# The mixer's input and output projections in pairs of column chunks, a quarter of their depth by seven products

## The chip, the cores and the metric

One core of one Trainium2 chip runs the kernel. The metric is the device time of one execution in microseconds. Before the change the median of three runs is 1919.73 us (1919.63 to 1920.5). One execution was also profiled; it took 1920.29 us, and the profiler's span of it is 1918.5 us.

Engines are named as in the profile: PE is the matrix engine (PEld its weight loads), DVE the vector engine, ACT the scalar engine, POOL the engine GpSimd, SP the queue that issues most transfers.

## The reference

A decoder layer on 256 tokens of width 2048 in float32:

```python
def reference(x, mem, ...):
    x = x + 0.5 * swiglu(rms_norm(x, ffn1_norm), ...)             # d_ff 5632
    x = x + hybrid_mixer(rms_norm(x, mix_norm), ...)
    x = x + cross_attention(rms_norm(x, xattn_norm), rms_norm(mem, mem_norm), ...)
    x = x + 0.5 * swiglu(rms_norm(x, ffn2_norm), ...)

def hybrid_mixer(h, ...):
    proj = h @ w_in                       # 2048 -> 6144 columns and 16 more
    qa, ka, va, qg, kg, vg, rg, glr = split(proj)
    qa = rope(rms_norm(heads(qa)) , pos) * HEAD_DIM ** -0.5
    ka = rope(rms_norm(heads(ka)), pos)
    o_attn = dilated_attention(qa, ka, heads(va))                  # 8 heads of 128
    o_gla = rms_norm(gla_chunked(qg, kg, vg, log_a)) * silu(rg)    # 4 heads
    return concatenate([o_attn, o_gla], axis=-1) @ w_out           # 2048 -> 2048
```

Accuracy is that of float32: the kernel splits each operand into a high part (rounded for the PE) and a low part (the rest), and adds three products, high by high, low by high and high by low.

## The kernel before

**Tiles.** Activations are held transposed, as tiles of 128 partitions x 4 x 256, one for 512 of the 2048 input columns; such a tile is called a k group, and there are four. A weight matrix is cut into column chunks of 512; one chunk of one k group is a load of 1 MB (`load`). ACT casts it to the high part `wh`, DVE subtracts to get the low part `wl` (`wsplit`; line 145 in the profile). A matmul multiplies 128x128 activations (the 256 tokens are two halves, t = 0 and 1) by 128x512 weights, so one chunk of one k group takes 24 matmuls: 4 rows of the group, 2 halves of the tokens, 3 products.

**Stages.** The two feed-forward stages and the middle (mixer and cross-attention) have separate memory pools. In the middle a load is split as two halves of 128x1024, with WB = 4 buffers for `wh` and as many for `wl`; in the feed-forward stages a load is split whole.

**Two ways to multiply.** `proj` (lines 175 to 177) takes one column chunk over its four k groups, 96 matmuls into two accumulators in PSUM. `strassen` (lines 219 and 184), used by the feed-forward stages alone, takes two column chunks at once. For two of the k groups the product of a 2x2 block matrix (two k groups by two chunks on the weights' side, two k groups by two token halves on the other) is formed by seven products rather than eight, from sums of weights and sums of activations (`sums_of`); the other k groups are added in the ordinary way (`whole`). The seven products run in a fixed order, P1 to P7. P1 goes into the tile `x`, P2 into `y`; ACT copies `x` to the first accumulator (`c0l`) and `y` to a tile `ys` in SBUF. P3 is added onto `x`, then DVE writes the accumulator `c0r = ys - x`. P4 is added to `c0l`. P5 is added onto `x`, so it has to wait until DVE has read `x`; then DVE writes `c1r = ys - x`. P6 is added to `c0r` and P7 onto `x`, again after that second reading.

**What sets the order.** A scheduler turns the program into a fixed list for each engine when the kernel is built; each engine works its list from the front. Weight loads and splits, and the copies and subtractions in `strassen`, are moved ahead of other work by 200 places where their operands and buffers allow. Steps between the projections (transposes, scores, softmax, attention) are put off with `later(n, step)`: each step runs after n ticks, and a tick is counted after half a k group in `proj`, after each product and twice in `whole`.

**Buffers.** [...] Short-lived tiles in SBUF, 2 KB in a partition each, come from one pool of SB = 6 buffers (`W2`): `ys`, and in the rotary step of a projection the tiles `sq`, `un`, `t1` and `t2`.

**The rotary step** (`roped`, lines 742 to 773, with `head_scale`, lines 448 to 462). For each token half of each query or key chunk, ACT squares the accumulator (`sq`), DVE reduces and scales it, POOL raises it to the power -1/2 (line 359), DVE multiplies (`qf` or `kf`), ACT scales the accumulator with it (`un`, four instructions), DVE and POOL make two products (`t2`, `t1`), DVE adds them (`qn`). Each instruction needs the one before.

The column chunks of `w_in` in the order worked on before: 6 and 7 (gated queries and keys), 8 and 9 (gated values), 10 and 11 (output gate), 0, 2, 1, 3 (query, key, query, key), 4 and 5 (values). The keys of the memory follow, then `w_out` in four chunks, k groups in the order 2, 3, 0, 1.

Of the kernel before, what the change touches and what calls it, by code (L numbers as in the profile page):

```python
# [29 lines left out]
WB = 4  # L30
PR0 = 10
PR1 = 9
ATT = 4
# [3 lines left out]
SCI = 1  # L37
ROPE = 8
XPRI = 170
MEM0 = 2  # L40
MEMS = 3
UB = 44
SB = 6
# [6 lines left out]
def layer_kernel(ctx: ExitStack, tc: tile.TileContext, A: dict, out: bass.AP):  # L50
# [144 lines left out]
    def new_sums():  # L195
        return tuple(FT(n, 1, [P, 2, 4, S], F32R, n) for n in ("sh", "sl"))

    def sums_of(ga, gb):

        t0, t1 = slice(0, P), slice(P, S)  # L200
        sums = new_sums()
        fa, fb = (FT("h", 8, [P, 4, S], F32, n) for n in ("fa", "fb"))
        for f, (h, l) in ((fa, ga), (fb, gb)):
            V.tensor_add(f, h.bitcast(F32), l.bitcast(F32))
        V.tensor_sub(fb[:, :, t1], fa[:, :, t1], fb[:, :, t1])
        V.tensor_sub(fa[:, :, t1], fa[:, :, t0], fa[:, :, t1])
        V.tensor_sub(fa[:, :, t0], fb[:, :, t1], fa[:, :, t0])
        V.tensor_add(fb[:, :, t0], fb[:, :, t0], fa[:, :, t0])
        for i, f in enumerate((fa, fb)):
            split(*(x[:, i] for x in sums), f)  # L210
        return sums

    def product(acc, lhs, w, start):

        wh, wl = w
        first = start
        for i, j, w in ((0, 0, wh), (1, 0, wh), (0, 1, wl)):
            for k in range(4):
                PE.matmul(acc, lhs(k)[i], w[:, k], start=first, stop=j == 1 and k == 3, skip_group_check=not start)  # L219
                first = False  # L220
        tick()

    def strassen(Wl, cl, Wr, cr, lhs, ab, sums, groups, mid=None, last=False):

        a, b = ab
        ral, rar = load(Wl, cl, a), load(Wr, cr, a)
        rbr, rbl = load(Wr, cr, b), load(Wl, cl, b)

        def parts(src):
            with tc.high_priority(WPRI):  # L230
                wh, wl = (FT(x, FWB, [P, 4, 512], F32R, x) for x in ("wh", "wl"))
                wsplit(wh, wl, src)
            return wh, wl
# [8 lines left out]

        def of(g, t):
            return lambda k: lhs(4 * g + k, t)

# [25 lines left out]
        if mid:  # L271
            mid()
        accs = ((c0l, x), (c0r, c1r))
        for i, g in enumerate(groups):
            end = i == len(groups) - 1
            for j, (acc, W, c) in enumerate(zip(accs, (Wl, Wr), (cl, cr))):
                if last and end and j:
                    both = [w for half in wgroup(W, c, g) for w in half]
                    for t in range(TT):
                        mm3(acc, lhs, both, False, True, (t,), seeded=True)  # L280
                    break
                both = [w for half in wgroup(W, c, g) for w in half]
                whole(acc, lhs, both, end)
                if i == j == 0:
                    product(x, of(b, 1), parts(ral), False)
# [360 lines left out]

    later(1, k_turn)
    later(3, gated_scores)
    later(4, kd_turn)

# [43 lines left out]

    for p2 in range(2):
        acc = proj(win, 8 + p2, lhs_x, range(4))
        for t in range(TT):
            SC.activation(vg[p2][t], acc[t], AF.Copy, scale=r2[:, t:t + 1])
        later(1, lambda p2=p2: states(p2))
        later(3, lambda p2=p2: outputs(p2))  # L700

# [12 lines left out]

    for p2 in range(2):
        acc = proj(win, 10 + p2, lhs_x, range(4))
        o2s = []
        for t in range(TT):
# [9 lines left out]
            o2s.append(o2)  # L728
        later(2, lambda p2=p2, o2s=o2s: gate_turn(p2, o2s))

# [11 lines left out]

    def roped(which, g, i, c):
        acc = proj(win, c, lhs_x, range(4))
        qns = []
# [26 lines left out]

        later(ROPE, turn)

# [44 lines left out]

    def values(g):  # L820
        acc = proj(win, 4 + g, lhs_x, range(4))
# [5 lines left out]
        later(ATT, lambda: attend(g, va))  # L827

# [5 lines left out]

    roped("q", 0, 0, 0)
    roped("k", 0, 1, 2)
    later(ROPE + SCD, lambda: scores(0, 0))
    later(ROPE + SCD + SCI, lambda: scores(0, 2))
    roped("q", 1, 0, 1)
    later(PR0, lambda: probs_turn(0))  # L840
    roped("k", 1, 1, 3)
    later(ROPE + SCD, lambda: scores(1, 0))
    later(ROPE + SCD + SCI, lambda: scores(1, 2))

# [61 lines left out]
    ss3 = new_ss("ss3")  # L906
    for c in range(NC):
        acc = proj(A["w_out"], c, lhs_m, (2, 3, 0, 1))
        for t in range(TT):
            V.tensor_add(xs[c][:, t], acc[t], xs[c][:, t])  # L910
        norm_chunk(c, xs[c], 32, ss3)
    r3 = rstd_of(ss3, "r3")
# [169 lines left out]
```

## Time and profile before

| | |
|---|---|
| median of the runs | 1919.73 us |
| profiled execution | 1920.29 us |
| its span | 1918.5 us |
| PE busy | 1890.5 us, 99% of the span |
| DVE busy | 1459.3 us, 76% |
| ACT busy | 1080.1 us, 56% |
| POOL busy | 125.7 us, 7% |
| the chain that ended last | PE 93%, DVE 4%, ACT 1% |
| mean granted PE clock | 0.995 |

The mixer and the cross-attention's projections lie between 713 and 1170 us of the span. In a row of a timeline the first number is the start in us, the second the time until the end of the last of the merged instructions; matmuls overlap, so the pace of a run of them is the difference of starts. In the rows of a table by windows each engine has its busy time and, in brackets, its instructions.

### The profile page before, as it was taken

The page shows a single profiled execution, that of the slowest core. Times are in us where ns is not written, and L with a number is a line of the kernel's source. Part 1 is how long each engine was busy: PE and PEld are TensorE (multiplying, and loading weights), DVE is VectorE, ACT ScalarE, POOL GpSimd, SP SyncE. Part 2 cuts the span into 40 slices and gives each one's busy share as a digit, 9 for nine tenths or more (in the row PEclk, how much of TensorE's full clock was granted, in tenths as well). Part 3 has the DMA queues.
Part 4 walks back from the last instruction along what each step waited for, and adds up shares of the span by engine and source line. Part 5 has one row for each costly group of instructions (what it writes and reads, how often), then busy time and mean ns, then how long its engine had stood idle before and what let it go on. Part 6 is the DMA issues. An engine that isn't in the chain of part 4 may idle for free.

```text
span 1918.5 us, 21566 instructions
## 1 busy us (share of the span) xinstructions
PE 1890.5 (99%) x8616; PEld 1563.4 (81%) x8616; DVE 1459.3 (76%) x1159; ACT 1080.1 (56%) x1028; POOL 125.7 (7%) x137
## 2 busy tenths in 40 slices
PE   8999999999999999999999999899999999999998
PEld 6888888888888778778888889788888888888876
DVE  7779887788888885446785555777888878888886
ACT  6556655555555556444676445555655556556553
POOL 2000000000000000002230000000000000000000
PEclk9999999999999999999999999899999999999999
DMA  9776787777877754445465554668768777787775
GB/s 376 274 244 225 241 301 280 275 240 241 277 246 274 250 157 174 169 158 194 174 221 200 195 193 157 254 198 293 231 230 285 259 275 272 246 284 233 242 253 171
DMA packets 68480, 453.90 MB, mean 237 GB/s; under 512 B 7675, under 2 KB 8827, under 8 KB 15004
## 3 DMA queue, kind: packets, MB, share of 16 engines
q1 hardware_dynamic: 56284, 370.74, 49.2%
q0 software_dynamic: 10944, 79.70, 18.5%
q10 hardware_dynamic: 1152, 2.10, 0.3%
q8 instruction: 67, 1.10, 0.2%
q14 instruction: 33, 0.27, 0.0%
HBM read 379.10 MB, written 6.29 MB: 201 GB/s over the span
## 4 chain that ended last, share of the span: by engine, by line
PE 93%; DVE 4%; issue 1%; ACT 1%; DMA 1%; POOL 0%; SPq 0%; DVEq 0%; POOLq 0%; ACTq 0%
PE acc L184 24%; PE x L219 17%; PE acc L176 9%; PE acc L177 9%; PE acc L175 9%; PE acc L219 9%; PE x L184 8%; PE y L219 4%; DVE wl L145 2%; ACT wh L145 1%; PE tp L383 1%; DVE raw L237 1%; DMA xr<-in_xT_dram 0%; DMA raw<-raw 0%; PE tp L343 0%
## 5 line engine op out<-in xcount | busy, mean ns | idle before, releaser
L145 DVE TENSOR_TENSOR wl<-raw,wh 128x2048 fp32r<-128x2048 f32 (+2 forms) x523 | 1013.6, 1954 | 367.1 <-ACT wh L145 366.7
L145 ACT CAST wh<-raw 128x2048 fp32r<-128x2048 f32 (+2 forms) x523 | 852.2, 1640 | 621.3 <-DVE raw L237 182.2
L175 PE MATMUL acc<-wh,xTh 128*128 128x512 f32 x544 | 216.3, 399 | 9.0 <-ACT wh L145 8.8
L176 PE MATMUL acc<-wl,xTh 128*128 128x512 f32 x544 | 214.9, 395 | 4.6 <-DVE wl L145 4.6
L177 PE MATMUL acc<-wh,xTl 128*128 128x512 f32 x544 | 214.2, 394 | 0.0
L237 DVE TENSOR_TENSOR raw<-raw 128x2048 f32<-128x2048 f32 x64 | 146.5, 2290 | 1.7
L241 POOL DMA_DIRECT2D raw<-raw x64 | 55.0, 860 | 1201.2 <-ACT sg L420 473.8
L175 PEld LDWEIGHTS acc<-wh,xTh 128*128 128x128 f32 x544 | 103.1, 190 | 32.4 <-ACT wh L145 10.5
L176 PEld LDWEIGHTS acc<-wl,xTh 128*128 128x128 f32 x544 | 103.6, 190 | 28.0 <-DVE wl L145 6.9
L184 PE MATMUL acc<-wl,xTh 128*128 128x512 f32 x480 | 121.8, 389 | 0.0
L184 PE MATMUL acc<-wh,xTl 128*128 128x512 f32 x480 | 121.8, 389 | 0.0
L184 PE MATMUL acc<-wh,xTh 128*128 128x512 f32 x480 | 121.8, 389 | 0.0
L177 PEld LDWEIGHTS acc<-wh,xTl 128*128 128x128 f32 x544 | 103.6, 190 | 21.7
L184 PEld LDWEIGHTS acc<-wl,xTh 128*128 128x128 f32 x480 | 90.1, 188 | 18.7
L184 PEld LDWEIGHTS acc<-wh,xTh 128*128 128x128 f32 x480 | 90.1, 188 | 18.7
L184 PEld LDWEIGHTS acc<-wh,xTl 128*128 128x128 f32 x480 | 90.1, 188 | 18.7
L219 PE MATMUL x<-wh,sh 128*128 128x512 f32 x256 | 71.2, 400 | 3.3 <-ACT wh L145 1.9
L219 PE MATMUL x<-wh,sl 128*128 128x512 f32 x256 | 68.8, 390 | 0.0
L219 PE MATMUL x<-wl,sh 128*128 128x512 f32 x256 | 68.7, 390 | 0.0
L420 ACT ACTIVATE sg<-acc,r 128x512 f32<-128x512 f32 x24 | 16.3, 689 | 84.7 <-PE acc L184 84.7
L184 PE MATMUL acc<-wh,hTl 128*128 128x512 f32 x232 | 59.2, 390 | 2.4 <-DVE hTl L303 2.4
L184 PE MATMUL acc<-wh,hTh 128*128 128x512 f32 x232 | 59.2, 390 | 0.9 <-ACT wh L145 0.9
(339 smaller groups left out, 2828.3 us busy)
## 6 DMA issues: line engine op xcount, KB each, us to landing
raw<-in_ffn_w_up_dram SPq DMA_DIRECT2D x88, 1024.0 KB, 8.9
raw<-in_ffn_w_down_dram SPq DMA_DIRECT2D x88, 1024.0 KB, 7.6
raw<-in_ffn_w_gate_dram SPq DMA_DIRECT2D x85, 1024.0 KB, 7.8
raw<-raw POOLq DMA_DIRECT2D x64, 1024.0 KB, 6.9
raw<-in_w_in_dram SPq DMA_DIRECT2D x48, 1024.0 KB, 4.8
raw<-in_w_out_dram SPq DMA_DIRECT2D x16, 1024.0 KB, 4.8
sl<-ffn_sl POOLq DMA_DIRECT2D x4, 1024.0 KB, 9.4
sh<-ffn_sh POOLq DMA_DIRECT2D x4, 1024.0 KB, 13.3
```

The costliest lines, as they stand in the source:

```text
L145: return SC.copy(wh, src), V.tensor_sub(wl, src, wh.bitcast(F32))
L175: PE.matmul(acc[t], lh, wh, start=first and i == 0, stop=False, skip_group_check=seeded)
L176: PE.matmul(acc[t], lh, wl, start=False, stop=False, skip_group_check=seeded)
L177: PE.matmul(acc[t], ll, wh, start=False, stop=last and i == len(half) - 1, skip_group_check=seeded)
L184: PE.matmul(acc[t], lhs(w[0], t)[i], w[1 + j], start=False, stop=last and j == 1 and n == len(group) - 1, skip_group_check=True)
L219: PE.matmul(acc, lhs(k)[i], w[:, k], start=first, stop=j == 1 and k == 3, skip_group_check=not start)
L237: V.tensor_add(dst, x, y)
L241: G.dma_start(dst, x, accum_op=ALU.add)
L383: PE.transpose(tp[:, j], hs[t][:, j * P:(j + 1) * P], ident)
L420: SC.activation(s, gate[t], AF.Silu, scale=r[:, t:t + 1])
```

## The change

Chunks of `w_in` are worked on in pairs by `strassen`: (8, 9), (10, 11), (0, 2), (1, 3), (4, 5); chunks 6 and 7 stay with `proj`. `w_out` is done in the pairs (0, 1) and (2, 3). Below these are the vg pair, the gate pair, the first and the second head pair, the value pair, the first and the second output pair. Unlike in the feed-forward stages, the 2x2 block matrix is made of the two halves of one k group, group 0, so each of the seven products has 6 matmuls; the other three groups follow with `whole`. P7 is done ahead of the first `whole` here. The activations' sums for `w_in` are made once, those for `w_out` from the attention's output of the first four heads. One of the additions of weights is made by an accumulating transfer, as in the feed-forward stages, the other three by DVE. `roped` and `values` get finished accumulators, four of them at the end of each pair, and the ticks of the later steps are set anew; the pool of long-lived tiles has 40 buffers rather than 44.

```diff
-PR0 = 10
-PR1 = 9
-ROPE = 8
+PROBS = 21
+ROPEQ = 9
+ROPEK = 12
-UB = 44
+UB = 40
...
     def strassen(Wl, cl, Wr, cr, lhs, ab, sums, groups, mid=None, last=False):
-        a, b = ab
-        ral, rar = load(Wl, cl, a), load(Wr, cr, a)
-        rbr, rbl = load(Wr, cr, b), load(Wl, cl, b)
+        large = phase["half_step"]
+        if large:
...
+        else:
+            rar, ral = load(Wr, cr, ab), load(Wl, cl, ab)
+            rbr, rbl = rar[:, 2:], ral[:, 2:]
+            rar, ral = rar[:, :2], ral[:, :2]
+            a, b, m = 4 * ab, 4 * ab + 2, 2
...
-        accumulate(ral, rbl)
+        if large:
+            accumulate(ral, rbl)
+        else:
+            add(ral, ral, rbl)
...
+        if not large:
+            product(x, of(b, 1), parts(ral), False)
         for i, g in enumerate(groups):
...
-    later(1, k_turn)
-    later(3, gated_scores)
-    later(4, kd_turn)
+    later(2, k_turn)
+    later(6, gated_scores)
+    later(7, kd_turn)
...
+    xsums = sums_of(*halves(*xT[0]))
+    def pair(cl, cr):
+        return strassen(win, cl, win, cr, lhs_x, 0, xsums, (1, 2, 3))
-    for p2 in range(2):
-        acc = proj(win, 8 + p2, lhs_x, range(4))
+    for p2, acc in enumerate(pair(8, 9)):
...
-    roped("q", 0, 0, 0)
-    roped("k", 0, 1, 2)
...
+    for g in range(2):
+        for i, acc in enumerate(pair(g, 2 + g)):
+            roped("qk"[i], g, i, acc)
+        later(ROPEK + SCD, lambda g=g: scores(g, 0))
+        later(ROPEK + SCD + SCI, lambda g=g: scores(g, 2))
+        later(PROBS, lambda g=g: probs_turn(g))
...
-    values(0)
-    later(PR1, lambda: probs_turn(1))
-    values(1)
+    for g, acc in enumerate(pair(4, 5)):
+        values(g, acc)
...
-    for c in range(NC):
-        acc = proj(A["w_out"], c, lhs_m, (2, 3, 0, 1))
+    msums = sums_of(mT[0, "h", 0], mT[0, "h", 2])
+    for c in range(0, NC, 2):
+        accs = strassen(A["w_out"], c, A["w_out"], c + 1, lhs_m, 0, msums, (2, 3, 1))
```

The lists of three engines at the start of the second head pair, right after the first head pair. Lines of the changed kernel stand some 15 to 20 further down than before: 451 is now 466, 750 is 770, 758 is 778, 219 is 220, and the copy to `ys` and the first subtraction, 260 and 264, are 270 and 274. Numbers behind a name tell one tile from another.

ACT, before, at the rotary step of chunk 0 (the accumulators are `acc_6015` for t = 0 and `acc_6016` for t = 1):

```order
L451 ACTIVATE sq_6171<-acc_6015 128x512
L145 CAST wh_6271<-raw_6253 128x1024
L750 ACTIVATE un_6182<-acc_6015,qf_6180 128x128 x4
L451 ACTIVATE sq_6194<-acc_6016 128x512
L145 CAST wh_6289<-raw_6287 128x1024
L145 CAST wh_6305<-raw_6287 128x1024
L750 ACTIVATE un_6205<-acc_6016,qf_6203 128x128 x4
L145 CAST wh_6323<-raw_6321 128x1024
```

ACT now, from the cast for P6 of the second head pair (`wh_6531`) on; `acc_6050` and `acc_6051` are the key accumulators of the first head pair, and `ys_6495` is the copy of P2 of the second:

```order
L145 CAST wh_6531<-raw_6463 128x1024
L145 CAST wh_6541<-raw_6465 128x1024
L145 CAST wh_6553<-raw_6551 128x1024
L770 ACTIVATE un_6405<-x_6047,qf_6403 128x128 x4
L466 ACTIVATE sq_6417<-acc_6050 128x512
L770 ACTIVATE un_6428<-acc_6050,kf_6426 128x128 x4
L466 ACTIVATE sq_6440<-acc_6051 128x512
L770 ACTIVATE un_6451<-acc_6051,kf_6449 128x128 x4
L270 COPY ys_6495<-y_6468 128x512
```

Before, at most one chunk's two rotary halves stood together in ACT's list, with casts between them. Now those of a query and a key chunk stand together, three of the four behind the casts of all products, and the copy to `ys` stands behind the last of them.

DVE now, at the same place; `acc_6470` is `c0r` of the second head pair:

```order
L476 TENSOR_SCALAR kf_6426<-kr_6424,r2_4798 128x4
L778 TENSOR_TENSOR t2_6435<-un_6428,tab_6037 128x4x64 x2
L468 TENSOR_REDUCE ks_6442<-sq_6440 128x4
L780 TENSOR_TENSOR qn_6438<-t1_6433,t2_6435 128x512
L471 TENSOR_SCALAR km_6444<-ks_6442,r2sq_4804 128x4
L472 TENSOR_SCALAR km_6444<-km_6444 128x4
L476 TENSOR_SCALAR kf_6449<-kr_6447,r2_4798 128x4
L778 TENSOR_TENSOR t2_6458<-un_6451,tab_6038 128x4x64 x2
L274 TENSOR_TENSOR acc_6470<-ys_6495,x_6467 128x512
```

The subtraction that makes `c0r` is new at this place and stands behind the rotary work of all four halves. On PE the list is P1, P2, P3, P4, two matmuls of the first `whole`, nine transposes of rotary results, and then P5 on `x_6467`, which needs that subtraction; everything later on PE stands behind P5.

More of the change, by code (lines that the diff above doesn't have):

```diff
@@ L195, in new_sums @@
     def new_sums():
-        return tuple(FT(n, 1, [P, 2, 4, S], F32R, n) for n in ("sh", "sl"))
+        return tuple(FT(n, 1, [P, 2, 4 if phase["half_step"] else 2, S], F32R, n) for n in ("sh", "sl"))
     def sums_of(ga, gb):
@@ L201, in sums_of @@
         sums = new_sums()
-        fa, fb = (FT("h", 8, [P, 4, S], F32, n) for n in ("fa", "fb"))
+        fa, fb = (FT("h", 8, [P, 4, S], F32, n) if phase["half_step"] else U([P, 2, S], F32, n) for n in ("fa", "fb"))
         for f, (h, l) in ((fa, ga), (fb, gb)):
@@ L217, in product @@
         for i, j, w in ((0, 0, wh), (1, 0, wh), (0, 1, wl)):
-            for k in range(4):
-                PE.matmul(acc, lhs(k)[i], w[:, k], start=first, stop=j == 1 and k == 3, skip_group_check=not start)
+            m = w.shape[1]
+            for k in range(m):
+                PE.matmul(acc, lhs(k)[i], w[:, k], start=first, stop=j == 1 and k == m - 1, skip_group_check=not start)
                 first = False
@@ L283, in strassen @@
                 whole(acc, lhs, both, end)
-                if i == j == 0:
+                if large and i == j == 0:
                     product(x, of(b, 1), parts(ral), False)
@@ L713, in gate_turn @@
             mT[2 + p2, t] = (hi, lo)
-    for p2 in range(2):
-        acc = proj(win, 10 + p2, lhs_x, range(4))
+    for p2, acc in enumerate(pair(10, 11)):
         o2s = []
@@ L741, in layer_kernel, with roped @@
     pn = {}
-    def roped(which, g, i, c):
-        acc = proj(win, c, lhs_x, range(4))
+    def roped(which, g, i, acc):
         qns = []
@@ L771, in turn @@
                 T[which, g, h0] = dst
-        later(ROPE, turn)
+        later(ROPEK if i else ROPEQ, turn)
     def scores(g, h0):
@@ L818, in attend, with values @@
             mT[g, "h", h0] = (hi, lo)
-    def values(g):
-        acc = proj(win, 4 + g, lhs_x, range(4))
+    def values(g, acc):
         va = []
@@ L826, in values @@
             va.append(v_)
-        later(ATT, lambda: attend(g, va))
+        later(ATT + 2 * g, lambda: attend(g, va))
     def lhs_m(k, t):
@@ L906, in layer_kernel @@
     ss3 = new_ss("ss3")
-    for c in range(NC):
-        acc = proj(A["w_out"], c, lhs_m, (2, 3, 0, 1))
-        for t in range(TT):
-            V.tensor_add(xs[c][:, t], acc[t], xs[c][:, t])
-        norm_chunk(c, xs[c], 32, ss3)
+    msums = sums_of(mT[0, "h", 0], mT[0, "h", 2])
+    for c in range(0, NC, 2):
+        accs = strassen(A["w_out"], c, A["w_out"], c + 1, lhs_m, 0, msums, (2, 3, 1))
+        for d, acc in zip((c, c + 1), accs):
+            for t in range(TT):
+                V.tensor_add(xs[d][:, t], acc[t], xs[d][:, t])
+            norm_chunk(d, xs[d], 32, ss3)
     r3 = rstd_of(ss3, "r3")
```

25 lines of the change are left out of this document (12 added, 13 removed).

## The prediction

> **What bounds the kernel now.** I read the page first (span, busy shares, chain), then the middle of the span by windows, since only that part changes.
>
> ```profile
> span 1918.5 us, 21566 instructions
> PE 1890.5 (99%) x8616; PEld 1563.4 (81%) x8616; DVE 1459.3 (76%) x1159; ACT 1080.1 (56%) x1028; POOL 125.7 (7%) x137
> PE 93%; DVE 4%; issue 1%; ACT 1%; DMA 1%; POOL 0%; SPq 0%; DVEq 0%; POOLq 0%; ACTq 0%
> 713.00:892.00 179.00, 178.65 (x839) 144.40 (x838) 96.88 (x115) 95.61 (x125) 13.14 (x14) 1.00 0.49 173
> 892.00:1040.00 148.00, 148.00 (x700) 124.01 (x699) 106.22 (x188) 95.22 (x168) 30.71 (x24) 1.00 0.56 199
> 1040.00:1085.00 45.00, 45.00 (x208) 37.44 (x207) 26.97 (x34) 23.62 (x37) 2.71 (x3) 1.00 0.50 188
> 1085.00:1170.00 85.00, 85.00 (x440) 72.89 (x439) 50.58 (x60) 43.33 (x61) 2.71 (x3) 1.00 0.53 186
> ```
>
> PE is the bound, and in the middle it has no gap at all: 456.65 of 457 us busy. DVE is busy for 281 of the same 457 us. So a matmul removed is time gained, one for one, and any wait that the change puts in front of PE is time lost, one for one.
>
> **The gain.** Seven pairs each replace 8 x 6 matmuls by 7 x 6, so 42 matmuls fewer, which is also the difference of the two programs' lists. Their pace:
>
> ```profile
> 706.28 1.98 PE L184 MATMUL acc<-wh,hTh 128*128 128x512 f32 x8
> 709.91 1.98 PE L184 MATMUL acc<-wl,hTh 128*128 128x512 f32 x8
> 916.41 1.03 PE L768 MATMUL tp<-ident,qn 128*128 128x128 f32 x8
> ```
>
> Sixteen matmuls start in 3.63 us, 0.227 us each: 42 x 0.227 = **9.5 us gained**. (Eight transposes take about 1.03 us, 0.13 each, used below.)
>
> [...]
>
> **What is added**, and whether DVE can carry it:
>
> ```profile
> L145 DVE TENSOR_TENSOR wl<-raw,wh 128x1024 fp32r<-128x1024 f32 x12 | 14.5, 1218 | 4.0 <-ACT wh L145 4.0
> L237 DVE TENSOR_TENSOR raw<-raw 128x2048 f32<-128x2048 f32 x64 | 146.5, 2290 | 1.7
> L264 DVE TENSOR_TENSOR acc<-ys,x 128x512 f32<-128x512 f32 x32 | 22.0, 688 | 2.0 <-PE x L219 2.0
> L345 DVE TENSOR_TENSOR xg<-tp,gain 128x512 f32<-128x512 f32 x24 | 16.0, 684 | 3.3 <-PE tp L343 3.3
> raw<-raw POOLq DMA_DIRECT2D x64, 1024.0 KB, 6.9
> ```
>
> A pair adds on DVE three weight additions (half of 2.29, say 1.15 each), three splits (1.22) and two subtractions (0.69): 8.5 us; ACT three casts and two copies. Seven pairs and the two sets of sums make about 68 us: 281 + 68 = 349 of 448. On average DVE isn't the bound. The accumulating transfer needs 6.9 us at twice the size and is wanted only at P5; it is hidden by P1 to P4 and the whole group ahead, and the loads through SP are the same in number.
>
> It is at the start of a pair that it matters. There PE takes 6 matmuls a product, 1.36 us, while DVE needs 1.7 us and more (13.4 for seven), and at that moment the previous pair's four accumulators come due together. So I followed each start by hand, along the lists of the engines, with the durations of the rows. Time 0 is when P1 could start; the first two accumulators of the pair before are ready one `whole` earlier, at -5.4.
>
> **The head pairs (the largest term).** The rotary step's chain, in the profile at chunk 0 (ACT, DVE, POOL in turn):
>
> ```profile
> 893.54 0.60 ACT L451 ACTIVATE sq<-acc 128x512 f32<-128x512 f32 x1 [0.36 <-PE acc L177]
> 896.88 1.14 ACT L750 ACTIVATE un<-acc,qf 128x128 f32<-128x128 f32 x4 [0.99 <-DVE qf L461]
> 903.98 1.14 ACT L750 ACTIVATE un<-acc,qf 128x128 f32<-128x128 f32 x4 [2.59 <-DVE qf L461]
> ...
> 898.06 1.86 DVE L758 TENSOR_TENSOR t<-un,tab 128x256 f32<-128x256 f32 x2
> 899.84 0.67 DVE L453 TENSOR_REDUCE qs<-sq 128x4 f32<-128x512 f32 x1
> 900.44 0.68 DVE L760 TENSOR_TENSOR qn<-t,t 128x512 f32<-128x512 f32 x1
> 901.04 1.21 DVE L145 TENSOR_TENSOR wl<-raw,wh 128x1024 fp32r<-128x1024 f32 x1
> 902.17 0.22 DVE L456 TENSOR_SCALAR qm<-qs,r2sq 128x4 f32<-128x4 f32 x1
> 907.73 3.49 DVE L145 TENSOR_TENSOR wl<-raw,wh 128x1024 fp32r<-128x1024 f32 x3
> ...
> 902.67 1.01 POOL L359 TENSOR_TENSOR qr<-qm,mhalf 128x4 f32<-128x4 f32 x1 [3.04 <-DVE qm L457]
> ```
>
> From the end of one `un` (898.02) to the end of the next (905.12) pass 7.1 us; without the split between them (1.13 from start to start) a round is 6.0. It is a chain of waits through three engines, and ACT's and DVE's lists hold nothing else there now. At the start of the second head pair DVE first has, from -5.3 on, eight splits (1.16), three additions (1.15), two reductions and one `qn` (0.6), one `t2` (1.87) and small ones (0.6): 17.1 us, with some waits done at about 12.5. Then the second query half's `un` ends at 15.4, the key's at 21.4 and 27.4, its `t2` at 29.3; only now comes the subtraction that frees `x`, done at 30.0. P5, and all of PE behind it, starts at 30.1. PE has by then 26 matmuls (5.9) and nine transposes (1.2) to do: **23 us stalled**. At the start of the value pair the lists read the same; score work replaces part of the early rotary work, the first `t2` starts at 11, the subtraction ends at 31.5, and PE has 7.5 us of work: **24 us**. Below, were nothing but the two key halves in the way (0.6 + 0.7 + 0.4 + 1.0 + 0.3 + 1.1, one round, `t2` and subtraction), P5 would start at 12.7 and 5.6 us be lost each time. Above, with a split in each round, 27.
>
> **The output pairs.** The first needs `msums`, and DVE makes them behind the memory keys' normalisation. From -0.4: two reductions, one addition, three splits, twice the small ones with POOL's power (1.7), two additions of 512 (0.6), four of 256 (0.36, half of the row of `xg` and a little) and a cast (0.6): done at 12.3. PE has P1 and P4 alone, 2.7: **10 us** (0 if the sums came before the keys' work, 11 with one more split). At the second, `c0r` stands behind four residual additions (0.68), three weight additions, eight splits, four `xg` and three low parts (0.68): 20.2 + 0.7 from -5.3, done at 15.6; PE has 24 + 2 matmuls and 16 transposes, 8.0: **7.5 us** (0 to 9).
>
> **The other three.** The vg pair waits for `xsums`, behind five splits, three additions and two products: the second sum is there at about 8, PE has 2.7: **5 us** (0 to 6). At the gate pair `c0r` comes after six splits and three additions, at 8.6 against 6.9, and the states' products wait another turn of splits: **3 us** (0 to 4). At the first head pair eight gate products of 0.6 push P7's split to 13 against 10.8: **3 us** (0 to 5).
>
> **The clock.** After a stall PE comes back at half speed:
>
> ```profile
> 1211.60 1.91 PE L343 MATMUL tp<-ident,x 128*128 128x128 f32 x16
> 1216.80 1.22 PE L175 MATMUL acc<-wh,xTh 128*128 128x512 f32 x2 [3.29 <-ACT wh L145]
> 1220.75 0.79 PE L176 MATMUL acc<-wl,xTh 128*128 128x512 f32 x1 [2.73 <-DVE wl L145]
> 1226.46 0.43 PE L175 MATMUL acc<-wh,xTh 128*128 128x512 f32 x1
> 1216.00:1220.00 4.00, 1.22 (x2) 0.50 (x2) 4.00 (x6) 2.83 (x4) 0.04 (x1) 0.54 1.02 430
> ```
>
> Between the starts at 1220.75 and 1226.46 lie 13 matmuls in 5.71 us instead of 2.95: 2.8 us lost. The two head stalls and the two at the output pairs are longer than the 3.29 us here: 4 x 2.8 = **11 us** (0 to 14).
>
> [...]
>
> **Sum.** -9.5 + 23 + 24 + 10 + 7.5 + 5 + 3 + 3 + 11 = +77. On the profiled execution's 1920.29 that is 1997; the median shown is 0.6 lower: **1996 us**. With all stalls at their lower ends, -9.5 + 11.2, no loss could be measured; I take the middle values because they are the lists' own order, and the low ends need DVE or ACT to do work in an order that their lists don't have.
>
> The moved steps cost what they did. Transposes and scores of the heads are 9 to 14 ticks on, inside the next pair; the memory's loads, 16 on SP, and their splits end inside the value pair, and the attention of the second four heads comes six ticks into the memory keys. Should that cover go, `attend` would stand in front of PE for its operands; I allow 0 to 10 us for it in the range alone.
>
> **Rivals.**
>
> *Only the rotary stalls.* The starts of the other five pairs hide behind splits made ahead, as the same scheme does in the feed-forward stages. Then -9.5 + 47 + 5.6 = +43: 1963 us. For it speaks this row of PE's waits:
>
> ```profile
> PE x L219 <- DVE acc L264: 0.8, 4, 0.2
> ```
>
> Thirty-two starts there cost P5 and P6 0.8 us in all. Against it: there a product has 12 matmuls, 2.7 us, and no sums are made in front of it. 20%.
>
> *Faster: every start hides.* If `ys` and the subtraction are ready when P3 is, as in that row, only the gain is left: 1920.3 - 9.5 = 1910.8, 1910 on the median. It decides from the point where all stalls together stay under 9.5 us. Against it stand the lists, in which the subtraction is behind four rounds of the chain. 5%.
>
> *Longer: attention comes late as well.* The head stalls push the scores, and the second four heads' attention meets the memory keys' end; another 15 to 20 us, about 2014. Against: six ticks of cover. 5%.
>
> *DVE becomes the bound of the whole middle*: 349 of 448 us busy says no; that the change doesn't do what it says: the 42 matmuls are gone from the list. 2% together, near no change.
>
> **How the numbers follow.** Forecast 68%, 1996 us, own range 1975 to 2014; the others as given. For eight in ten I reach down past 1963 to 1955 and up to 2015. A measurement of this kernel can tell 0.2%, some 4 us, from no change: slower than that 93%, within it 2%, faster 5%.
>
> **What would show it.** In the new trace PE should have two idle stretches of over 20 us altogether, after the first and the second head pair, released by DVE's subtraction (line 274), with ACT's `ys` copy directly behind the last `un`; one of about 10 us at the first output product with sums, released by ACT's cast to `sh`; smaller ones at the other starts; and the granted clock near 0.5 behind each. 42 matmuls fewer at 0.227. I'm wrong if PE's P5 in the head pairs starts within 10 us of P4, if the middle is as full as before, or if PE comes back from the stalls at full speed.

## The result, and the profile after

The changed kernel takes 2004.16 us (median of 4 runs, 2002.29 to 2006.06) against 1919.68 us of the kernel before on the same chip (4 runs, 1918.78 to 1920.5): a ratio of 1.044, 95% interval 1.0422 to 1.0458. The forecast was 1996 us, slower. The profiled execution took 2002.29 us, its span is 2000.5 us, 82.0 more than before.

The page of the changed kernel: span, busy shares, the chain that ended last.

```profile
span 2000.5 us, 21720 instructions
PE 1903.0 (95%) x8574; PEld 1564.1 (78%) x8574; DVE 1523.0 (76%) x1231; ACT 1108.2 (55%) x1067; POOL 138.0 (7%) x144
PE 84%; DVE 8%; ACT 3%; issue 2%; DMA 1%; POOL 1%; SPq 0%; ACTq 0%; DVEq 0%; POOLq 0%
```

PE has 42 instructions fewer, as foretold, and is still busy for 12.5 us more: that alone says that it ran slower for a while. The middle, cut by windows (PE, weight loads, DVE, ACT, POOL, granted clock):

```profile
766.00:800.00 34.00, 25.13 (x110) 19.72 (x111) 25.74 (x31) 17.03 (x21) 0.00 (x0) 0.85 0.43 140
800.00:875.00 75.00, 75.00 (x326) 57.51 (x326) 37.72 (x40) 36.30 (x55) 2.91 (x3) 1.00 0.48 164
930.00:975.00 45.00, 24.35 (x93) 18.31 (x92) 30.82 (x41) 18.92 (x35) 10.94 (x9) 0.73 0.32 106
1000.00:1048.00 48.00, 25.41 (x101) 19.35 (x100) 32.68 (x53) 24.80 (x48) 18.35 (x13) 0.72 0.34 116
1107.00:1131.00 24.00, 14.91 (x62) 11.26 (x61) 18.04 (x28) 14.30 (x23) 2.01 (x2) 0.86 0.29 95
```

The first row is the start of the vg pair, the second holds the start of the gate pair without a gap, the next two are the starts of the second head pair and of the value pair, the last that of the first output pair. With the last 748.5 us of both spans set apart, the middle from 713 on lasts 539 us instead of 457. Between the same two instructions, the first matmul of line 175 (at 713.45 before, 712.23 now) and the first of the cross-attention's scores (at 1172.48 and 1255.50), it lasts 84.2 us longer; the stages ahead and behind are 2.2 us shorter this time.

PE's timeline at the starts; in square brackets the idle time ahead and what ended it. The rows at 931.57, 1003.65, 1107.52 and 1162.02 are P1 of four pairs.

```profile
771.39 1.22 PE L220 MATMUL acc<-wh,xTh 128*128 128x512 f32 x2 [5.66 <-ACT acc L264]
777.76 0.49 PE L220 MATMUL x<-wh,sh 128*128 128x512 f32 x1 [3.45 <-ACT sh L145]
...
887.89 1.22 PE L220 MATMUL x<-wh,sh 128*128 128x512 f32 x2 [3.38 <-ACT acc L264]
...
931.57 0.62 PE L220 MATMUL x<-wh,xTh 128*128 128x512 f32 x2
...
947.54 0.48 PE L788 MATMUL tp<-ident,qn 128*128 128x128 f32 x1 [4.09 <-ACT un L770]
...
959.86 0.47 PE L788 MATMUL tp<-ident,qn 128*128 128x128 f32 x1 [7.72 <-ACT ys L270]
961.86 1.22 PE L220 MATMUL x<-wh,sh 128*128 128x512 f32 x2 [1.52 <-DVE acc L274]
...
1003.65 0.62 PE L220 MATMUL x<-wh,xTh 128*128 128x512 f32 x2
...
1020.79 0.90 PE L822 MATMUL tp<-ident,pc 128*128 128x128 f32 x3 [8.07 <-ACT un L770]
1033.11 0.90 PE L822 MATMUL tp<-ident,pc 128*128 128x128 f32 x3 [11.42 <-ACT ys L270]
1035.11 0.80 PE L220 MATMUL x<-wh,sh 128*128 128x512 f32 x1 [1.10 <-DVE acc L274]
...
1107.52 0.62 PE L220 MATMUL x<-wh,mTh 128*128 128x512 f32 x2
...
1119.78 0.79 PE L220 MATMUL x<-wh,sh 128*128 128x512 f32 x1 [7.88 <-ACT sh L145]
...
1162.02 0.61 PE L220 MATMUL x<-wh,mTh 128*128 128x512 f32 x2
...
1172.79 1.09 PE L358 MATMUL tp<-ident,x 128*128 128x128 f32 x4 [4.50 <-DVE xg L360]
```

Added up with the smaller ones, PE is idle for 71.7 us in the middle: 9.1 at the vg pair, 0 at the gate pair, 4.1 and 20.6 at the two head pairs, 22.6 at the value pair, 9.1 and 5.9 at the output pairs, 0.3 elsewhere. Why it is so late at the second head pair stands in ACT's timeline there:

```profile
946.34 1.14 ACT L770 ACTIVATE un<-x,qf 128x128 f32<-128x128 f32 x4 [4.17 <-DVE qf L476]
952.27 1.14 ACT L770 ACTIVATE un<-acc,kf 128x128 f32<-128x128 f32 x4 [4.30 <-DVE kf L476]
...
958.19 1.14 ACT L770 ACTIVATE un<-acc,kf 128x128 f32<-128x128 f32 x4 [4.30 <-DVE kf L476]
959.21 0.60 ACT L270 COPY ys<-y 128x512 f32<-128x512 f32 x1
```

The rounds of the rotary chain follow each other at 5.9 us, and the copy to `ys`, whose operand P2 left in PSUM at about 934.5, comes straight behind the last `un`, 25 us later. Little of PE's idle time there is ended by the subtraction of line 274 itself (1.5 us here, 1.1 at the value pair). Most lies at the transposes ahead of P5, and the last of those wait for the copy to `ys` too (7.7 and 11.4 us), though they don't read `ys`. They write to a buffer in PSUM, one of four of the kernel's pool `pm`, from which `x` and `y` come too, so it must be the one of `y` that they wait for; that is inferred.

### The profile page after: what moved, and what is told of

Its sections match the earlier page's. It is cut to its first block, busy times and chain, and to the rows that moved or that the text cites. A ratio compares the mean times of both kernels' runs of the same rounds, so it can differ in the third digit from the quotient of the medians.

```text
span 2000.5 us, 21720 instructions
## 1 busy us (share of the span) xinstructions
PE 1903.0 (95%) x8574; PEld 1564.1 (78%) x8574; DVE 1523.0 (76%) x1231; ACT 1108.2 (55%) x1067; POOL 138.0 (7%) x144
## 3 DMA queue, kind: packets, MB, share of 16 engines
q0 software_dynamic: 11952, 83.37, 18.8%
## 4 chain that ended last, share of the span: by engine, by line
PE 84%; DVE 8%; ACT 3%; issue 2%; DMA 1%; POOL 1%; SPq 0%; ACTq 0%; DVEq 0%; POOLq 0%
PE acc L184 30%; PE x L220 18%; PE x L184 10%; PE acc L220 9%; PE y L220 4%; DVE wl L145 3%; PE acc L176 3%; PE acc L177 3%; PE acc L175 3%; ACT wh L145 2%; DVE raw L247 2%; PE tp L398 1%; DVE t L778 1%; DMA raw<-raw 1%; DMA xr<-in_xT_dram 1%
## 5 line engine op out<-in xcount | busy, mean ns | idle before, releaser
L247 DVE TENSOR_TENSOR raw<-raw 128x2048 f32<-128x2048 f32 (+1 forms) x85 | 173.0, 2036 | 2.0
L184 PE MATMUL acc<-wh,xTh 128*128 128x512 f32 x660 | 170.6, 392 | 2.8 <-ACT wh L145 2.8
L184 PE MATMUL acc<-wl,xTh 128*128 128x512 f32 x660 | 168.2, 390 | 0.0
L184 PE MATMUL acc<-wh,xTl 128*128 128x512 f32 x660 | 167.5, 389 | 0.0
L184 PEld LDWEIGHTS acc<-wh,xTh 128*128 128x128 f32 x660 | 123.7, 188 | 29.1 <-ACT wh L145 3.6
L184 PEld LDWEIGHTS acc<-wh,xTl 128*128 128x128 f32 x660 | 123.9, 188 | 25.8
L184 PEld LDWEIGHTS acc<-wl,xTh 128*128 128x128 f32 x660 | 123.7, 188 | 25.9 <-issue 0.4
L220 PE MATMUL x<-wh,sh 128*128 128x512 f32 x284 | 83.7, 411 | 21.7 <-ACT sh L145 11.3
L175 PE MATMUL acc<-wh,xTh 128*128 128x512 f32 x224 | 89.3, 403 | 6.2 <-ACT wh L145 6.2
L176 PE MATMUL acc<-wl,xTh 128*128 128x512 f32 x224 | 90.0, 402 | 5.1 <-DVE wl L145 5.1
L177 PE MATMUL acc<-wh,xTl 128*128 128x512 f32 x224 | 89.4, 399 | 0.0
L220 PEld LDWEIGHTS x<-wh,sh 128*128 128x128 f32 x284 | 51.8, 192 | 36.3 <-ACT sh L145 12.5
L220 PEld LDWEIGHTS x<-wl,sh 128*128 128x128 f32 x284 | 53.9, 191 | 12.3 <-DVE wl L145 1.0
L220 PEld LDWEIGHTS x<-wh,sl 128*128 128x128 f32 x284 | 54.2, 191 | 11.7
L435 ACT ACTIVATE sg<-acc,r 128x512 f32<-128x512 f32 x24 | 16.3, 689 | 84.7 <-PE acc L184 84.7
```

The source lines that it names most:

```text
L175: PE.matmul(acc[t], lh, wh, start=first and i == 0, stop=False, skip_group_check=seeded)
L176: PE.matmul(acc[t], lh, wl, start=False, stop=False, skip_group_check=seeded)
L177: PE.matmul(acc[t], ll, wh, start=False, stop=last and i == len(half) - 1, skip_group_check=seeded)
L184: PE.matmul(acc[t], lhs(w[0], t)[i], w[1 + j], start=False, stop=last and j == 1 and n == len(group) - 1, skip_group_check=True)
L247: V.tensor_add(dst, x, y)
L435: SC.activation(s, gate[t], AF.Silu, scale=r[:, t:t + 1])
```

## The experiments

All times are medians of four runs, each beside runs of the kernel before on the same chip. From each kernel's profiled execution the table also has PE's idle time in the middle, the time there at a granted clock of 0.50 (the middle cut into windows of 0.25 us) and half of PE's busy time in it, an estimate of what half speed cost. Where an edit adds lines of code, the later ones stand further down: line 247 is 251 in the kernels with early sums.

| kernel | us | against before | PE idle | at half speed | lost by it |
|---|---|---|---|---|---|
| changed kernel | 2004.2 | +84.5 | 71.7 | 78.5 | 16.1 |
| `ys` in its own buffer | 1991.0 | +71.4 | 53.1 | 68.3 | 22.6 |
| head chunks one by one | 1964.2 | +44.6 | 35.7 | 41.0 | 12.5 |
| output chunks one by one | 1985.1 | +65.5 | 55.3 | 64.9 | 14.2 |
| own `ys`, raw copies | 1975.6 | +56.0 | 43.4 | 44.4 | 13.6 |
| sums early | 1989.9 | +70.8 | 56.8 | 68.3 | 16.7 |
| raw copies alone | 1987.7 | +68.6 | 51.9 | 61.4 | 17.4 |
| all mended | 1947.4 | +28.3 | 18.8 | 23.9 | 11.0 |
| POOL's work moved | 1937.6 | +18.8 | 17.1 | 13.7 | 4.6 |
| four pairs | 1936.5 | +17.8 | 14.0 | 13.7 | 5.0 |
| ticks set anew | 1946.0 | +26.1 | 20.5 | 27.3 | 11.0 |

### The buffer of `ys`

```diff
-UB = 40
+UB = 39
-            ys = W2([P, 512], "ys")
+            ys = W2([P, 512], "ys") if large else FT("ys", 1, [P, 512], F32, "ys")
```

> The changed kernel, but the copy ys has a buffer of its own instead of one of the six short-lived ones (the long-lived pool has 39 buffers instead of 40; that alone leaves every engine's list as it was). Theory: the stalls at the second head pair and the value pair (20.6 and 22.6 us of idle PE) exist because ys needs a buffer that the rotary step of the fourth half frees, so that the subtraction of line 274 stands behind all four rounds. With its own buffer P5 needs only the accumulator of the first half, and what is left is the wait of the second subtraction for the third half, some 8 us at each start: 2004.2 - 12.6 - 14.6 - 5 of half speed = about 1972 us. Rival: the four accumulators themselves are freed too late by the chain of rounds, and the place of ys is only a symptom. Then another wait takes over, the two idle stretches keep 17 us and more each, and the time stays at 1995 us or above.

1991.02 us, ratio 1.0368 (1.0353 to 1.0384). The buffer is a cause: idle PE falls to 10.6 us at the second head pair and 10.2 at the value pair. At the second head pair the copy to `ys` and then P5 now come here (P1 starts at 931.51):

```profile
936.29 0.62 ACT L270 COPY ys<-y 128x512 f32<-128x512 f32 x1
```

```profile
941.17 0.71 PE L220 MATMUL x<-wh,sh 128*128 128x512 f32 x2
```

What is left in PE's timeline:

```profile
959.14 1.22 PE L220 MATMUL x<-wh,xTh 128*128 128x512 f32 x2 [3.91 <-DVE acc L282]
...
1021.31 1.22 PE L220 MATMUL x<-wh,xTh 128*128 128x512 f32 x2 [5.42 <-DVE acc L282]
...
1106.68 0.80 PE L220 MATMUL x<-wh,sh 128*128 128x512 f32 x1 [10.69 <-ACT sh L145]
```

P7 now waits for the second subtraction (line 282), which needs the accumulator of the third rotary half: the wait foretold by the theory. But the time fell by 13 us and not by 32. The first output pair's wait for its sums grew by 2.8 us, and a new one of 2.0 us came up at the memory keys; and half speed costs 6.5 us *more* although PE is idle 18.6 us less: more of PE's work now falls into the slow stretches (45.2 us of it, twice the 22.6, against 32.2). The size was wrong, the rival (1995 us and above) too.

### The head chunks one by one

```diff
-        for i, acc in enumerate(pair(g, 2 + g)):
-            roped("qk"[i], g, i, acc)
+        for i in range(2):
+            roped("qk"[i], g, i, proj(win, 2 * i + g, lhs_x, range(4)))
```

with the ticks of the kernel before for the transposes and scores (8, 9, 10), and 18 for the attention's transposes.

> The changed kernel, but the four query and key chunks go through proj one by one as before; vg, gate, value and output pairs stay. Theory: the rotary work of four accumulators at once is what costs; the first and second head pair's stalls (4.1 and 20.6 us) go, the value pair keeps a wait for the two halves of one key chunk, some 6 us instead of 22.6, about 10 us of half speed go, and two pairs' gain of 1.4 us each is lost: 2004.2 - 4.1 - 20.6 - 16.6 - 10 + 2.7 = about 1956 us. Rival: a pair's own start (three additions and seven splits on DVE) costs what it costs whatever stands ahead; then the value pair keeps 15 us and more, and the time is 1970 us or above.

1964.24 us, ratio 1.0231 (1.0216 to 1.0246), 40 us less than the changed kernel. With the head chunks no wait above 0.25 us is left. The value pair, now behind one key chunk, keeps 10.9 us, most of it in this row:

```profile
994.87 0.90 PE L822 MATMUL tp<-ident,pc 128*128 128x128 f32 x3 [6.81 <-ACT ys L270]
```

The wait for `ys` is still there with two rotary halves ahead instead of four. The theory holds but for this, which it had at 6 us, and the time is 8 us above its 1956.

### The output chunks one by one

```diff
-    msums = sums_of(mT[0, "h", 0], mT[0, "h", 2])
-    for c in range(0, NC, 2):
-        accs = strassen(A["w_out"], c, A["w_out"], c + 1, lhs_m, 0, msums, (2, 3, 1))
+    for c in range(NC):
+        acc = proj(A["w_out"], c, lhs_m, (2, 3, 0, 1))
```

> The changed kernel, but the four chunks of w_out go through proj as before; all input pairs stay. Theory: the output pairs' stalls (9.1 and 5.9 us, with some 4 us of half speed behind them) are their own: the sums of the attention's output for the first, the residual additions and the norm for the second. They go, two gains of 1.4 us are lost: 2004.2 - 15 - 4 + 2.7 = about 1988 us. Rival: these stalls are handed down from the attention that comes late after the head pairs, and proj would wait there as well: 1998 us or above.

1985.08 us, ratio 1.034 (1.0323 to 1.0357): 19.1 us less than the changed kernel, 16 foretold. With `proj` no wait above 0.25 us is left there; the output pairs' stalls are their own.

### Own `ys`, and raw copies of the accumulators

The edit of `ys` above, and in the rotary step:

```diff
+            qn = U([P, 4, HD], F32, "qn")
+            with tc.high_priority(WPRI):
+                SC.copy(flat, acc[t])
-            f = head_scale(acc[t], r2, r2sq, t, ...)
+            f = head_scale(flat, r2, r2sq, t, ...)
...
             V.tensor_add(qn, t1, t2.rearrange("p h s d -> p h (s d)"))
+            for h in range(4):
+                SC.activation(qn[:, h], qn[:, h], AF.Copy, scale=f[:, h:h + 1])
```

where `flat` is `qn` in two dimensions.

> As the first kernel of this set (ys has its own buffer), and the rotary step first copies the raw accumulator to SBUF with one ACT copy of 128x512, ahead of other work; squares and rotary products read that copy, and the normalising factor is applied at the end instead of the beginning. The arithmetic is the same but for the order of two multiplications; each half has one ACT copy more. Theory: both reasons for the late P5 and P7 (the buffer of ys, and accumulators held for whole rounds) are gone, the second head pair and the value pair lose nearly all their 43 us of idle PE and some 8 us of half speed: about 1957 us. Rival: DVE's own work at a pair's start (13.4 us for the weights of seven products against 9.5 us of PE) holds P5 to P7 whatever the accumulators do; then 5 us and more stay at each start and the time is 1965 us or above.

1975.56 us, ratio 1.0291 (1.0276 to 1.0306). The second head pair keeps 3.6 us of idle PE, the value pair's P1 to P7 0.9. Then comes another wait:

```profile
1021.67 0.90 PE L790 MATMUL tp<-ident,qn 128*128 128x128 f32 x3 [6.70 <-ACT qn L782]
```

Transposes of the rotary result stand in PE's list where the finished result is not there yet, with `whole` behind them. So neither theory nor rival is whole: the two reasons for the late P5 and P7 were right, and the chain, still as long, met PE at its next customer; the time is above the rival's 1965, but not for its reason. The wait for the output sums again grew, to 10.82 us.

### Raw copies alone

The edit of the rotary step without that of `ys`.

> The changed kernel with the raw copy of the accumulators alone (squares and rotary products read a copy in SBUF, the factor is applied at the end), ys stays in the pool of six short-lived buffers. It parts the two reasons that the fourth kernel took away together (1975.6 us; ys alone 1991.0). Theory: both are needed: the short-lived buffers turn over with the rotary rounds, three per half, and ys is still the thirteenth request behind the first, so P5 still stands behind the rounds; gain under 15 us: 1990 us or above. Rival: with the accumulators copied the rounds are short enough that ys gets its buffer in time, and the time is within 4 us of the fourth kernel's, about 1976 us.

1987.72 us, ratio 1.0357 (1.0342 to 1.0373). This edit alone gains 16.4 us, that of `ys` alone 13.1, both 28.6: near the sum, 29.6. In idle PE they overlap more: 18.6 and 19.8 us less alone, 28.3 together. Neither the theory's 1990 nor the rival's 1976 came. At the second head pair (P1 at 932.79) the copy to `ys` and P5 come here:

```profile
949.61 0.56 ACT L270 COPY ys<-y 128x512 f32<-128x512 f32 x1
```

```profile
952.23 1.22 PE L220 MATMUL x<-wh,sh 128*128 128x512 f32 x2
```

Behind P1 there, P5 and P7 start after:

| kernel | P5, us | P7, us |
|---|---|---|
| changed kernel | 30.3 | 35.0 |
| `ys` in its own buffer | 9.7 | 27.6 |
| raw copies alone | 19.4 | 24.0 |
| both | 9.6 | 13.7 |

So P5 is late for the buffer of `ys`, which the shorter hold of the accumulators frees only in part; with that mended, P7 is late for the accumulators. The two are not links of which both are needed, as the theory had it.

### The sums early

The sums for `w_in` are made after the gated queries. Those for `w_out` are made right behind the value pair, of k group 2:

```diff
-        accs = strassen(A["w_out"], c, A["w_out"], c + 1, lhs_m, 0, msums, (2, 3, 1))
+        accs = strassen(A["w_out"], c, A["w_out"], c + 1, lhs_m, 2, msums, (3, 0, 1))
```

> The changed kernel, but the sums of activations are made earlier: those for w_in after the gated query chunk instead of after the gated keys, those for w_out from k group 2 (the gate's output, ready long before) instead of group 0, with the order of the groups 2, 3, 0, 1. Nothing else differs. Theory: the waits for the sums (3.45 us of idle PE at the vg pair, 7.88 us at the first output pair, both released by the cast to sh) go, and with them some 5 us of half speed: about 1988 us. Rival: the sums are only the last of what DVE is late with; the same products then wait for the splits or for ACT's copy to the first accumulator, and the time is 1997 us or above.

1989.93 us, ratio 1.0368 (1.0352 to 1.0383), as the theory had it. At the first output pair nothing waits for the sums any more, 1.2 us ahead of the memory keys' transposes are left of 9.1, and the vg pair keeps 3.6 of 9.1.

### All mended

Besides all edits above: POOL's product with the output gain is made on the attention's output during the gate pair, DVE's gate products are put off by four ticks, and

```diff
-        later(ROPEK if i else ROPEQ, turn)
+        later((ROPEK + 4 * g) if i else ROPEQ + 3 * g, turn)
...
-            norm_chunk(d, xs[d], 32, ss3)
+            norm_chunk(d, xs[d], 32, ss3, 1 if c else 9)
```

with the second heads' scores four ticks later too.

> The changed kernel with all the mends together: ys in its own buffer, raw copies of the accumulators in the rotary step, both sets of sums early, POOL's product with the output gain made on the attention's output ahead of the next pair and DVE's gate products put off by four ticks, the rotary transposes and scores of the second heads three and four ticks later, the norm's transposes of the first output pair nine ticks later instead of one. All seven pairs stay. Theory: each stall is one of order, and none is the price of seven products as such; what is left is some 2 to 4 us at each of four starts and one or two windows of half speed: 1919.6 - 9.5 + 12 + 5 = about 1927 us. Rival: at a pair's start the in-place sums of weights are a chain of their own (cast, split, addition, about 3.4 us a product against 1.4 of PE), so that each of the seven starts keeps 4 us and more with half speed behind: 1945 us or above.

1947.41 us, ratio 1.0143 (1.0126 to 1.016). Two thirds of the loss are gone, and still it is just above the rival's 1945. The output pairs and the gate pair start with 2.7 us of idle PE in all; the vg pair has 3.6, the head pairs 2.4 and 3.6, and 3.1 stand ahead of the second scores. At the first head pair, DVE's timeline and then POOL's:

```profile
870.84 4.40 DVE L756 SCALAR_TENSOR_TENSOR o<-og,orr,sr 128x256 f32<-128x256 f32 x3
```

```profile
872.12 2.83 POOL L770 TENSOR_TENSOR tab<-tab,gb 128x512 f32<-128x512 f32 x2
```

DVE's three gate products are not alike (the least, median and longest time of one, in ns):

```profile
L756 DVE SCALAR_TENSOR_TENSOR o<-og,orr,sr x3: 476/478/3607, 870.8 to 871.6; 128x256 f32<-128x256 f32 x3
```

The last of them, begun at 871.6, takes 3.61 us instead of 0.48 and ends 0.3 us behind the two products with which POOL scales the rotary tables.

### POOL's work moved

The tables are scaled at the start of the middle, the rotary product `t1` is DVE's, the gated keys' transposes come a tick later, the second scores and the attention's transposes three ticks. The attention of the second four heads comes a tick later too.

> All mends of the kernel before (1947.4 us, 18.8 us of idle PE left), and three more: the rotary tables are scaled by POOL at the start of the middle stage and not at the start of the first head pair; the rotary product that POOL made is made by DVE; the gated keys' transposes come one tick later, the second heads' scores three and their attention's transposes three. In the trace of the kernel before, three gate products on DVE took 4.40 us together while POOL scaled the tables, against some 1.2 us otherwise. Theory: at the starts of the first and second head pair it is POOL that holds DVE up; the 2.4 and 3.6 us of idle PE there shrink by two thirds, the 1.9 and 3.1 us of the transposes and scores go: about 9 us of idle PE and 6 us of half speed: 1919.4 - 9.5 + 9 + 6 = about 1925 us. Rival: POOL's work only happens to lie there, and DVE's own list at a pair's start is too long; then moving more onto DVE makes it worse: 1945 us or above.

1937.55 us, ratio 1.0101 (1.0086 to 1.0116), between the two. DVE's row at the same place:

```profile
868.00 1.27 DVE L763 SCALAR_TENSOR_TENSOR o<-og,orr,sr 128x256 f32<-128x256 f32 x3
```

4.40 us have become 1.27, the first head pair starts without a gap (2.4 before), the second with 0.95 (3.6). What held the one product of 3.61 us in the kernel with all mends is not shown: by the profile it had started 0.5 us ahead of POOL's first product (871.6 against 872.12). But two new waits came up, on PE and, behind the first, on POOL:

```profile
1015.88 1.12 PE L801 MATMUL tp<-ident,qn 128*128 128x128 f32 x4 [4.61 <-ACT qT L803]
...
1054.70 1.51 PE L835 MATMUL tp<-ident,pc 128*128 128x128 f32 x6 [5.11 <-DVE mTl L322]
```

```profile
1011.73 2.95 POOL L344 TENSOR_TENSOR xr<-xr,gain 128x512 f32<-128x512 f32 x2 [6.97 <-DMA xr<-in_memT_dram]
```

ACT's copies of the rotary queries stood behind a cast of a memory tile, which stood behind POOL, which waited for that tile's transfer. The second wait is for DVE's split of the attention's output.

### Four pairs

The vg and head chunks one by one, with the mends that still apply.

> Only four of the seven pairs are left, those whose starts showed little idle PE once mended (gate, value, both output pairs); vg and the head chunks go one by one as before. All mends that still apply are kept (ys in its own buffer, raw copies, sums early, output gain early, norm's transposes later, tables early, rotary product on DVE). Theory: four pairs gain 24 matmuls, 5.4 us, and some 4 us of idle PE with 2 to 3 us of half speed are left: 1919.4 - 5.4 + 7 = about 1921 us, no difference that can be told. Rival: with the accumulators of the heads freed in twos the starts hide altogether and the gain shows: 1915 us or less.

1936.51 us, ratio 1.0094 (1.0077 to 1.0111), 15 us above the theory. The starts of the four pairs have 2.1 us of idle PE, but 4.7 stand ahead of rotary transposes and 4.1 ahead of those of the memory's keys. Probably these are ticks set for other lengths; no run of four pairs tests it.

### The ticks set anew

All seven pairs; the memory's loads at ticks 1, 3, 5, 7 and their splits six ticks later, the rotary transposes one to four ticks later than in the changed kernel, the tables scaled during the gated keys.

> All seven pairs with the mends of the eighth kernel (1937.6 us, 17.1 us of idle PE in the middle), but the tables are scaled during the gated keys rather than at the very start, the rotary transposes come one to four ticks later, the scores of the second heads two ticks earlier and their attention's transposes two ticks earlier than there, and the memory's loads start a tick earlier, two ticks apart instead of three, with six ticks instead of three to their splits. In the eighth kernel's trace 4.61 us of idle PE stood behind POOL's product on a memory tile that had just landed, and 5.11 us behind the attention's split. Theory: these two waits and 2.2 us of a rotary transpose are only ticks set for other lengths, since seven of a pair's nineteen ticks are half as long; they go, with two windows of half speed: 1918.8 - 9.5 + 6 + 5 of restarts and drained pipelines = about 1921 us. Rival: each mend of the ticks only moves the wait to the next engine; 1932 us or above.

1945.96 us, ratio 1.0134 (1.0117 to 1.0151): worse than the kernel it was made from, and the rival is right. The wait for `qT` is 4.77 us again. ACT's timeline ahead of it:

```profile
1013.39 1.28 ACT L793 ACTIVATE qn<-qn,kf 128x128 f32<-128x128 f32 x4 [3.38 <-DVE qn L791]
...
1017.50 1.65 ACT L345 CAST memh<-xr 128x512 fp32r<-128x512 f32 x3
1019.06 0.57 ACT L803 COPY qT<-tp 128x512 f32<-128x512 f32 x1
```

The copy stands behind seven casts, five of memory tiles among them, and these behind the last factor of the rotary keys, which waits for DVE. The vg pair is back at 4.31 us. DVE's additions of weights at that start (line 251 here):

```profile
763.60 1.23 DVE L251 TENSOR_TENSOR raw<-raw 128x1024 f32<-128x1024 f32 x1
...
767.27 1.22 DVE L251 TENSOR_TENSOR raw<-raw 128x1024 f32<-128x1024 f32 x1
...
770.95 1.23 DVE L251 TENSOR_TENSOR raw<-raw 128x1024 f32<-128x1024 f32 x1
```

They come 3.67 us apart: each sum is written over the last, so it waits for the split of the last, which waits for its cast, which waits for the sum. PE needs 1.36 us for a product. At the vg pair the chain begins 1.9 us ahead of P1. At the gate pair, where it begins 4.4 us ahead and twelve of the states' products lie between P2 and P3, nothing waits.

No version here beats the kernel before; seven products are worth 9.5 us, and the smallest loss seen was 21.7 us with four pairs (16.3 us of span, and their 5.4 of gain).

## Why the prediction was right

It was right in sign and size, and its largest terms came by its own steps. The clock's term was too small (11 us, at most 14, against 16.1), and the vg pair's stall came by another chain. The single stalls missed by 3 us too many to 4.1 too few and partly cancelled (75.5 foretold, 71.4 measured), so that the sum lies nearer than its terms: that part is luck.

**The gain** is 42 matmuls, as the page shows.

**The second head pair and the value pair.** The prediction had P5 30.1 us after P1 at the first and 31.5 at the second. The rows give 961.86 - 931.57 = 30.3 and 1035.11 - 1003.65 = 31.5. The mechanism is as told, with rounds of 5.9 us (6.0 foretold) and `ys` behind the last `un`. The stalls are 20.6 and 22.6 us, not 23 and 24, because PE did its work in between partly at half speed (granted clock 0.50 from 942.00 and from 1013.68 on) and so waited less; that part is in the clock's term. That the buffer of `ys` is the reason for the late P5 is shown by the first kernel, where P5 starts 9.7 us after P1. What then holds P7 are the accumulators, as the fourth shows.

**The output pairs.** The sums of the first were to be there 12.3 us after P1: 1119.78 - 1107.52 = 12.3; 9.1 us idle against 10. The steps that it lists add up to 12 us or a little more and begin at -0.4, so the last half microsecond of that agreement is luck. The second has 5.9 against 7.5. The kernel with output chunks one by one shows that both belong to the pairs.

**The vg pair, 5 us foretold, 9.1 measured.** The walk had the sums at about 8 us after P1 and P4 as work done meanwhile. ACT there:

```profile
767.34 1.04 ACT L145 CAST wh<-raw 128x1024 fp32r<-128x1024 f32 x1 [2.63 <-DVE raw L247]
...
770.75 0.58 ACT L264 COPY acc<-x 128x512 f32<-128x512 f32 x1
...
773.50 1.04 ACT L145 CAST wh<-raw 128x1024 fp32r<-128x1024 f32 x1 [1.55 <-PE acc L220]
777.09 0.62 ACT L145 CAST sh<-fa 128x512 fp32r<-128x512 f32 x1 [2.55 <-DVE fa L207]
```

P4 needs the copy to `c0l`, which stands on ACT behind a cast that waits for an addition of weights; the next cast waits until P4 gives its buffer back, and only behind that cast and its split come the sums. Two waits in a row, where the walk had one beside the other. The first head pair's 4.1 us (3 foretold) end the same way, with this copy, and not with P7's split. The gate pair's 3 us did not come.

**The clock, 11 us foretold.** This is the term that was mis-sized. The span grew by 82.0; 71.4 of idle PE more than before less 9.5 leave 20.1 us. Half of PE's busy time at half speed is 16.1 of them: seven stretches at a granted clock of 0.50, 78.5 us together, in which PE is busy for 32.2. The prediction counted four stalls of 2.8 us from one place in the trace of before. In fact there are seven stretches, the half speed goes on during a stall with the little work in it, and one such piece:

```profile
938.50:942.10 3.60, 1.36 (x7) 0.78 (x5) 3.60 (x4) 1.92 (x2) 0.00 (x0) 0.99 0.00 0
942.10:965.90 23.80, 7.75 (x20) 5.18 (x21) 14.29 (x26) 6.96 (x19) 7.33 (x6) 0.50 0.23 89
965.90:970.00 4.10, 4.10 (x20) 3.38 (x19) 3.20 (x3) 2.11 (x2) 0.00 (x0) 1.00 0.53 174
```

holds the second head pair's whole start. The other 4.0 us are not placed by any row (6.2 in the middle, since the stages around it are 2.2 shorter). A likely part, worked out and not shown: idle time is counted from the end of the last matmul, which lies some 0.17 us behind the moment at which the next could have started (a single matmul is 0.39 us long in the timeline, at a pace of 0.227), and there are 23 waits, 3.9 us together.

**The rivals.** *Only the rotary stalls* (1963 us) is refuted by the vg and the output pairs, whose starts do not hide; its row of waits came from products of twice the length. (That row is of P5 alone: P6, which the prediction names with it, doesn't write to `x`.) *Every start hides* and *attention late as well* did not come: the attention's own products wait for nothing above 0.25 us after the value pair. DVE was not the bound on average: in the stretch from 942.10 to 965.90 above it is busy for 14.29 of 23.80 us and ACT for 6.96, since the rounds of a chain leave each engine waiting for the next.

The 8 us between forecast and result are 5 of the clock and 4 that are not placed, less 4 of stalls foretold too long, and about 3 that lie between the profiled execution and the median, now and before.

## What to carry to other kernels

Seven products instead of eight are worth one product's time each (1.36 us here), so price a pair's start first: the serial chain of sums, casts and splits, the accumulators that come due together, and every short-lived buffer taken from a pool that slow work turns over. A copy that PE will need should not draw its buffer from the pool of a long chain. And where PE stalls, count the time at half speed behind and within the stall apart from the stall; a mend that only shortens waits can give back less than it saves: with `ys` in its own buffer PE was idle for 18.6 us less, and the time fell by 13.1.

## What the runs showed of the hardware

**In these traces half speed came in whole windows of 3.41 us, at a phase of their own.** The stretches at 0.50 in the changed kernel are 6.83, 3.42, 3.42, 23.89, 27.31, 6.83 and 6.82 us long: 2, 1, 1, 7, 8, 2 and 2 times 3.41. They begin whole windows apart as well: from 767.92 on at 778.16, 887.39 and 942.00, which are 3, 35 and 51 windows. The experiments' totals at half speed, 13.7 to 68.3 us, are 4 to 20 of them. The vg pair has the same two waits (5.66 and 3.45 us, equal to 0.02) in the changed kernel and in the first four experiments, but 10.25, 13.65, 13.66, 6.83 and 13.65 us at half speed. In one place the slow window lay wholly behind the wait: in the first experiment's kernel, after an idle time of 3.38 us that ended at 887.98:

```profile
885.00:888.80 3.80, 0.82 (x3) 0.67 (x4) 3.80 (x7) 2.40 (x3) 1.27 (x1) 0.99 0.65 198
888.80:892.10 3.30, 3.30 (x9) 2.38 (x8) 3.05 (x4) 2.48 (x4) 3.30 (x2) 0.50 0.00 0
892.10:895.00 2.90, 2.82 (x13) 2.13 (x13) 2.90 (x3) 2.23 (x3) 1.50 (x1) 0.99 0.00 0
```

PE first worked at full speed, then a full window at half. So a stall's cost moved from kernel to kernel with no change at that place: half of PE's busy time in the vg pair's stretches is 3.2, 4.4, 4.4, 3.1 and 4.3 us in those five. The wider spread of the changed kernel's runs (3.8 us against 1.7) may come from this; no run shows it. The prediction took its 2.8 us for a stall from 5.71 us between two rows. Read by windows, that place in the trace of before is one stretch of 10.24 us:

```profile
1216.30:1226.54 10.24, 7.01 (x16) 5.03 (x17) 10.24 (x11) 7.37 (x7) 0.46 (x1) 0.50 1.01 401
```

That is three windows for two waits (3.29 and 2.73 us), and the 5.71 us lie within them; what the prediction was missing was the number of windows.

**Beside POOL's products, a product on DVE took 3.61 us instead of 0.48.** With POOL's work moved, three products of 128x256 took 1.27 us with no POOL product beside them; in the kernel with all mends they took 4.40 us, beside two of POOL's that took 2.83. The whole difference lies in one of the three.
